# A hybrid S5, short convolution and attention layer on one core: S5 yields given other lengths, q and k requested by the work in front of them

## The chip, the core and the metric

The kernel runs on one core of a Trainium2 chip. The engines that matter here are TensorE (PE in the rows; PEld is its loading of weights), VectorE (DVE), ScalarE (ACT), GpSimd (POOL) and SyncE (SP, which here mostly starts DMAs). Each engine takes its own list of instructions in order and waits on semaphores for what the others make. The metric is device time in microseconds (us) of one execution, lower is better. TensorE's clock is granted at one of two levels, 1.2 or 2.4 GHz; the profile shows the mean of a stretch as PEclk, 1.00 for the upper level.

## The reference

One layer over 1024 tokens of width 1024, in float32:

```python
def hybrid_layer(x, ...):
    h = rmsnorm(x, g_pre_mix)
    proj = jnp.einsum('bld,dn->bln', h, w_in)          # 1024 -> 6664 columns
    u_s5, x_conv, b_conv, c_conv, q, k, v, f_logit, gate_logits = split(proj)
    y_a = s5_mixer(u_s5, ...)            # 32 groups x 16 channels, 64 complex states each
    y_b = gate_b * conv3_causal(gate_c * x_in)
    y_c = forgetting_attention(q, k, v, f_logit, b_f)  # 8 heads x 64, blocks of 128 queries
    gates = jax.nn.sigmoid(gate_logits + b_gate)       # 3 x 1024 columns
    merged = sum over the three branches of gate * (y @ its rows of w_branch)
    x = x + rmsnorm(merged @ w_out, g_post_mix)
    h = rmsnorm(x, g_pre_mlp)
    return x + rmsnorm(square(relu(h @ w_ff1)) @ w_ff2, g_post_mlp)

def s5_mixer(u, ...):
    states = associative_scan(a_bar, b_bar * u)        # complex, over the tokens
    y = gelu(Re(c * states) + d_skip * u)
    return y * sigmoid(y @ w_glu)
```

## The kernel before

Everything that TensorE multiplies from float32 is split by `split` (L71) into a high and a low part in the type fp32r: ScalarE copies the high part, VectorE subtracts it (the copy at L73 and the subtraction at L65 in the rows), and `mm3` multiplies three pairs (high with high, high with low, low with high), each one a product of 128x512 at L122. A projection tile (128 columns of `w_in`) is 2 halves of tokens x 8 blocks of depth x `mm3`, 48 products.

The order of TensorE's work is written by a small planner in Python that runs while the kernel is built. Chains of dependent work are generators (`s5_all` for the S5 branch, `attention`, `forget`, `w2_sums`); where one `yield`s a number, it asks to be called again after so many modelled microseconds. `clk` is a modelled clock, moved on by each matmul that is issued. `run_with` (L106) calls whichever chain is due, and fills in between with one step of `proj_stream` (L263), which is one `mm3` of a projection tile. A modelled `mm3` lasts 0.64. The tiles stand in the queue `todo`: first 12 of the short convolution (cx, cc and cb for each of four blocks j), then 22 gate tiles (g0 to g21), then what is put at its head while the program goes on. The first steps of a tile's stream ask SP for the weights of the tiles behind it, and `nxt.split()` splits the next tile's weight between the steps of this one: `if nxt is not None and (th, kt) == (0, 5):` (L285).

The S5 branch is done in four quarters j of 8 groups (`s5_quarter`, L700 to L825). In one quarter: `Bt` is made of small products by VectorE and GpSimd (Bx) and added up; eight transposes of it (pm, L126) give Mi; `CA` is made in the same way with Cx; `pk` multiplies Bb with CA and gives, through Kq and DMAs, Wi; GpSimd then makes the tables TR and TI of the next quarter (`s5_tables`; those of quarter 0 are asked for ahead of the first quarter); `px` multiplies Mi with U; VectorE makes X of px and of the tables TR and TI, then the scans Z (eight instructions); ScalarE copies Z to Zs; VectorE makes S of Z, Zs and the tables; `py` multiplies CA with S and Wi with U; after a gelu (G1, gq) `pz` multiplies, and so goes to memory as `ya_s`. The yields between them set how much filler stands ahead of each step:

```python
yield SY * (3.9 if j else 9.0)     # L723, ahead of Bt's sum and pm
yield SY * (3.9 if j else 13.0)    # L740, ahead of CA's sum and pk
yield SY * 15.0                    # L790, ahead of py
```

When the quarters are done, what is left of the convolution and one gate tile is issued, then v (pv, the weights of v split by hand), and then the attention. Its 64 units are 4 pairs of heads (hp) x 2 heads x 8 blocks of queries; each has its scores (ps), a softmax on VectorE and ScalarE (P), transposes (pt, to PT), and for every second block the product with v (av). Between these stand the fillers that are left. The q and k tiles of the next pair are put at the head of `todo` by `request_qk`, and the planner issues them behind the last scores of the pair in front (`ready` in `proj_stream`):

```python
if n % 16 == 12 and hp < 3:        # L1114
    request_qk(hp + 1)
```

Beside the attention run GpSimd's sums of `w_ff2` (`w2_sums`), with a row of DMAs on SP. In this stage SP keeps the program's order. Outside the stages that are marked as scheduled by hand, the compiler's scheduler may reorder the instructions of each engine.

Of the kernel before, what the change touches and what calls it, by code (L numbers as in the profile page):

```python
# [38 lines left out]
def hybrid_layer(ctx, tc, a, out, dbg=None):  # L39
# [24 lines left out]
    def tt(o, x, y, op, eng=None):  # L64
        (eng or dve).tensor_tensor(o, x, y, op=op)  # L65
# [27 lines left out]
    clk = [0.0]  # L93
# [4 lines left out]
    def spawn(gen, delay=0.0):  # L98
        heapq.heappush(events, (clk[0] + delay, seq[0], gen))
        seq[0] += 1  # L100

    def poll():
        while events and events[0][0] <= clk[0]:
            _, _, gen = heapq.heappop(events)
            d = next(gen, None)
            if d is not None:  # L106
                spawn(gen, d)
# [146 lines left out]
    def proj(tl, th):  # L254
        wh, wl = tl.split()
        ps = pp.tile([P, HALF], F, name=f"p_{tl.name}{th}", tag="pj", bufs=2)
        for kt in range(KT):
# [2 lines left out]
                tl.cons(th, ps)  # L260
            yield

    def proj_stream():  # L263
        nxt = None
        while True:
            if nxt is None and not todo:
                yield DONE
                continue
            cur = nxt if nxt is not None else todo.popleft()
            cur.split()  # L270
            nxt = todo.popleft() if todo else None
            if nxt is not None:
                nxt.raw.get()
                if cur.name in ahead_of:
                    ahead_of[cur.name].get()
                elif todo:
                    todo[0].raw.get()
            while cur.ready is not None and not cur.ready():
                if not events:
                    raise RuntimeError("stuck")  # L280
                clk[0] = max(clk[0], events[0][0])
                poll()
            for th in range(2):
                for kt, _ in enumerate(proj(cur, th)):
                    if nxt is not None and (th, kt) == (0, 5):  # L285
                        nxt.split()
                    yield


# [381 lines left out]
    SY = 1  # L671
# [28 lines left out]
    def s5_quarter(j):  # L700
# [17 lines left out]
        for s in range(T):  # L718
# [1 line left out]
            e2 = pii[:, T - 1 - s, gs].unsqueeze(2).to_broadcast([P, 8, H])  # L720
            tt(Bt[:, :, s, :], Bb[:, gs, :], e1, MUL)
            tt(Bx[:, :, s, :], Bb2[:, gs, :], e2, MUL, pool)
        yield SY * (3.9 if j else 9.0)  # L723
        tt(Bt, Bt, Bx, ADD)
        yield SY * 2.4
        Mi = q4("Mi", "D")
# [8 lines left out]
        for tau in range(T + 1):  # L735
# [1 line left out]
            e2 = pii2[:, tau, gs].unsqueeze(2).to_broadcast([P, 8, H])  # L737
            tt(CA[:, :, tau, :], C1t[:, gs, :], e1, MUL)
            tt(Cx[:, :, tau, :], C2t[:, gs, :], e2, MUL, pool)
        yield SY * (3.9 if j else 13.0)  # L740
        tt(CA, CA, Cx, ADD)
        yield SY * 2.4

# [43 lines left out]
        tt(Zs[:, :, 0:nv], Zs[:, :, 0:nv], TI[:, :, 0:nv], MUL)  # L787
        tt(S[:, :, 1:P], S[:, :, 1:P], Zs[:, :, 0:nv], SUB)

        yield SY * 15.0  # L790
        py = pp.tile([P, 8, P], F, name=f"py{j}", tag="s", bufs=2)
        for g in range(8):
            mm(py[:, g, :], CA[:, g, 1:T + 1, :].rearrange("p t h -> p (t h)"),
# [98 lines left out]
    for grp in (1, 0):  # L892
        n = 264 if grp else 256
# [131 lines left out]
    def request_qk(hp):  # L1025
        tl = tiles(f"q{hp}", [(C_Q + hp * P, P), (C_K + hp * P, P)], 2, qk_cons(hp),
                   ready=lambda: sdone.get(hp - 1, False))
        todo.extendleft(reversed(tl))

    def attention():  # L1030
# [3 lines left out]
        def scores(u):  # L1034
            hp, e, qb = u
            h = 2 * hp + e
            Q1, Q2, K1, K2 = QK[hp, e]
            kend = (qb + 1) * P
            nch = 1 if kend <= 512 else 2
            cw = kend // nch  # L1040
            mw = max(256, cw)
            qs = slice(qb * P, (qb + 1) * P)
            ps = pp.tile([P, 2, 512], F, name=f"ps{h}{qb}", tag="s", bufs=2)
            for c in range(nch):
                ks = slice(c * cw, c * cw + mw)
                last = c == nch - 1
                mm(ps[:, c, 0:mw], Q1[:, qs], K1[:, ks], True, False, 0.000417 * mw)
                mm(ps[:, c, 0:mw], Q2[0:68, qs], K2[0:68, ks], False, not last, 0.000417 * mw)
                if last:
                    mm(ps[:, c, cw - P:cw], identb, maskb, False, True, 0.06)  # L1050
            sv = ps[:, 0:nch, 0:cw]
            mx = at.tile([P, 1], F, name=f"mx{h}{qb}", tag="mx", bufs=4)
            dve.tensor_reduce(mx, sv, axis=mybir.AxisListType.XY, op=MAX, negate=True)  # L1053
            Pm = Pms[u] = at.tile([P, L], F, name=f"P{h}{qb}", tag="P", bufs=3)
            sm = at.tile([P, 1], F, name=f"sm{h}{qb}", tag="sm", bufs=4)
            act.activation(Pm[:, 0:kend].rearrange("p (c n) -> p c n", c=nch), sv, AF.Exp,  # L1056
                           bias=mx, accum_out=sm)
            dve.reciprocal(sm, sm)
            ts(Pm[:, 0:kend], Pm[:, 0:kend], sm, MUL)
# [43 lines left out]
                av_(u)  # L1103

        prev = None
        for n, u in enumerate(units):
            hp = u[0]
            if n % 16 == 0:
                if hp == 0:
                    request_qk(0)  # L1110
                while not sdone.get(("qk", hp)):
                    yield 1.3
                yield 4.0
            scores(u)  # L1114
            if n % 16 == 15:
                sdone[hp] = True
            yield FILL_A
            if prev is not None:
                yield from tail(prev)
            if n % 16 == 12 and hp < 3:  # L1120
                request_qk(hp + 1)
            prev = u
        yield 3.0
        yield from tail(prev)
# [743 lines left out]
    for i in range(0, KC, 2):  # L1868
        nxt = [p.prep_a for p in pairs[i + 2:i + 4]] if i + 2 < KC else [s_[0] for s_ in stages[:AH]]
# [65 lines left out]
```

## Time and profile before

| | us |
|---|---|
| three runs | 1651.32, 1644.12, 1651.83 |
| median | 1651.32 |
| the profiled execution | 1648.08 |
| span of its instructions | 1646.3 |
| TensorE busy | 1603.7 (97%) |
| VectorE busy | 1033.7 (63%) |
| ScalarE busy | 702.9 (43%) |
| GpSimd busy | 460.8 (28%) |

All times in the rows count from the start of the span. The four S5 quarters lie between about 90 and 350 us, v behind them, the attention between about 460 and 815, and the branch products, the output projection and the MLP after it. In a row of instructions, "x8" is the number of like instructions put together, and the bracket at the end is the idle time of the engine just before, with what ended it.

### The profile page before, as it was taken

Reading aid. Unit: us, or ns where it says so; the run is one execution under the profiler, and the core shown is the slowest. Engines: PE = TensorE matmul, PEld = TensorE weight load, DVE = VectorE, ACT = ScalarE, POOL = GpSimd, SP = SyncE. Lnnn points to the kernel's source line nnn. Section 1 sums busy time; section 2 is a strip of 40 time slices with the busy share of each in tenths; the row PEclk is TensorE's granted clock in tenths of the full one; section 3 lists DMA queues with packets and bytes.
Section 4 is the critical chain, followed back from the end, with each engine's and each line's share of the span. In section 5 each row is a group of like instructions: output and inputs, shape, how many; then the busy total and the mean of one; then the engine's idle time right before and its main releaser. Section 6 shows DMA issues by size and latency. Waiting matters only on the chain.

```text
span 1646.3 us, 20948 instructions
## 1 busy us (share of the span) xinstructions
PE 1603.7 (97%) x7783; PEld 1322.8 (80%) x7783; DVE 1033.7 (63%) x1543; ACT 702.9 (43%) x1060; POOL 460.8 (28%) x578
## 2 busy tenths in 40 slices
PE   7999999999999999999999989999999999999997
PEld 6778888889878888777887768888788878888886
DVE  4768666524156463677682874978887674545665
ACT  6223233322254454566343344744445454443442
POOL 1087844100231413120002314444433200101232
PEclk9999999999999999999999999999999999999999
DMA  5412323332463526441873672456554699665521
GB/s 166 125 46 77 105 76 111 91 103 64 145 214 111 196 96 202 131 167 62 282 253 110 216 241 90 149 173 198 184 175 146 202 344 358 236 202 187 186 88 51
DMA packets 186034, 261.73 MB, mean 159 GB/s; under 512 B 24752, under 2 KB 108764, under 8 KB 183884
## 3 DMA queue, kind: packets, MB, share of 16 engines
q1 hardware_dynamic: 170380, 228.93, 43.2%
q10 hardware_dynamic: 15552, 31.46, 5.1%
q8 instruction: 61, 1.00, 0.2%
q14 instruction: 41, 0.34, 0.1%
HBM read 183.54 MB, written 75.63 MB: 157 GB/s over the span
## 4 chain that ended last, share of the span: by engine, by line
PE 42%; DVE 7%; issue 3%; DMA 3%; ACT 3%; POOL 2%; SPq 0%; DVEq 0%; ACTq 0%; POOLq 0%
PE P L122 13%; PE P4f L122 3%; PE P6f L122 3%; PE P7f L122 3%; PE P5f L122 3%; PE P2f L122 3%; PE P3f L122 3%; PE P1f L122 2%; PE wl L122 2%; PE p_g L122 2%; DVE sa L65 1%; PE p_q L122 1%; PE ps L122 1%; PE av L122 1%; PE pt L126 1%
## 5 line engine op out<-in xcount | busy, mean ns | idle before, releaser
L65 DVE TENSOR_TENSOR st<-x,st 128x1024 fp32r<-128x1024 f32 x70 | 86.8, 1251 | 78.5 <-ACT st L73 77.0
L122 PE MATMUL p_g<-hT,w_g_1H 128*128 128x512 f32 x384 | 125.6, 403 | 0.0
L122 PE MATMUL p_g<-hT,w_g_0H 128*128 128x512 f32 x384 | 124.2, 401 | 1.2 <-ACT K L1019 1.2
L73 ACT ACTIVATE st<-x 128x1024 fp32r<-128x1024 f32 x70 | 73.6, 1059 | 99.0 <-PE P6f L122 16.6
L65 POOL TENSOR_TENSOR w2s<-w2s 128x512 f32<-128x512 f32 x32 | 44.5, 1390 | 215.7 <-DMA w2s<-in_w_ff 188.4
L65 POOL TENSOR_TENSOR s<-w1r 128x512 f32<-128x512 f32 x32 | 53.8, 1701 | 145.5 <-DMA w1r<-in_w_ff 114.9
L65 DVE TENSOR_TENSOR sl<-x,sh 128x1024 fp32r<-128x1024 f32 x42 | 56.6, 1352 | 47.4 <-ACT sh L73 47.4
L122 PEld LDWEIGHTS p_g<-hT,w_g_0H 128*128 128x128 f32 x384 | 69.7, 189 | 13.5 <-ACT K L1019 1.6
L122 PE MATMUL pb<-yH,wb_0L 128*128 128x512 f32 x192 | 75.5, 393 | 3.6 <-DVE wb_0L L65 3.6
L122 PEld LDWEIGHTS p_g<-hT,w_g_1H 128*128 128x128 f32 x384 | 69.4, 190 | 11.6 <-issue 0.2
L122 PE MATMUL p_g<-hT,w_g_1L 128*128 128x512 f32 x192 | 75.8, 395 | 0.0
L122 PE MATMUL p_g<-hT,w_g_0L 128*128 128x512 f32 x192 | 75.5, 393 | 0.0
L65 POOL TENSOR_TENSOR fa<-fa,gfin 128x512 f32<-128x512 f32 x16 | 25.5, 1604 | 178.3 <-ACT fjk L1762 178.3
L122 PE MATMUL pb<-yH,wb_0H 128*128 128x512 f32 x192 | 75.2, 392 | 0.0
L122 PE MATMUL pb<-yL,wb_0H 128*128 128x512 f32 x192 | 74.8, 390 | 0.0
L65 DVE TENSOR_TENSOR PT<-pt,PT 128x512 fp32r<-128x512 f32 (+2 forms) x96 | 53.1, 553 | 28.9 <-ACT PT L73 28.4
L73 ACT ACTIVATE PT<-pt 128x512 fp32r<-128x512 f32 (+2 forms) x96 | 46.9, 489 | 53.5 <-PE pt L126 52.4
L73 ACT ACTIVATE sh<-x 128x1024 fp32r<-128x1024 f32 x42 | 44.2, 1058 | 51.4 <-PE P3f L122 9.9
L1056 ACT ACTIVATE P<-ps,mx 128x128 f32<-128x128 f32 (+3 forms) x64 | 47.3, 739 | 28.1 <-DVE mx L1053 28.0
L1053 DVE TENSOR_REDUCE mx<-ps 128x1 f32<-128x128 f32 (+3 forms) x64 | 48.1, 751 | 13.6 <-PE ps L122 13.3
L862 ACT ACTIVATE g<-p_g,bgcol 128x512 f32<-128x512 f32 x48 | 32.8, 682 | 45.8 <-PE p_g L122 45.3
L126 PE MATMUL pt<-ident,P 128*128 128x128 f32 x288 | 48.7, 278 | 3.0 <-DVE PT L65 2.3
(810 smaller groups left out, 4568.0 us busy)
## 6 DMA issues: line engine op xcount, KB each, us to landing
w2s<-in_w_ff SPq DMA_DIRECT2D x16, 1024.0 KB
w1r<-in_w_ff SPq DMA_DIRECT2D x16, 1024.0 KB
as<-sa SPq DMA_DIRECT2D x16, 1024.0 KB
x<-as SPq DMA_DIRECT2D x32, 512.0 KB
x<-t_P SPq DMA_DIRECT2D x32, 512.0 KB
r_g<-in_w_in SPq DMA_DIRECT2D x12, 1024.0 KB
gt_s<-g ACTq DMA_DIRECT2D x48, 256.0 KB
t_P<-w2s SPq DMA_DIRECT2D x48, 256.0 KB
```

What stands on the lines that cost most here:

```text
L65: (eng or dve).tensor_tensor(o, x, y, op=op)
L73: act.activation(hi, src, AF.Copy, scale=scale)
L122: pe.matmul(o, l, r, start=start, stop=stop)
L126: pe.transpose(o, i, idn)
L862: act.activation(g, ps, AF.Tanh, bias=bgcol[:, i:i + 1], scale=0.5)
L1053: dve.tensor_reduce(mx, sv, axis=mybir.AxisListType.XY, op=MAX, negate=True)
L1056: act.activation(Pm[:, 0:kend].rearrange("p (c n) -> p c n", c=nch), sv, AF.Exp, bias=mx, accum_out=sm)
```

## The change

Four places are edited. The yield ahead of pm is 15.0 instead of 9.0 in quarter 0; that ahead of pk is 8.0 instead of 13.0 in quarter 0 and 1.5 instead of 3.9 in the others; that ahead of py is 10, 15, 13 and 11 in quarters 0 to 3 instead of 15 in each. `proj_stream` splits the weight of a next tile that has a `ready` condition and a raw weight of its own (a q tile behind a gate tile) in its second half of tokens instead of its first. And the attention measures how long its own units last in the modelled clock, and requests q and k when the filler that is left in the tile at hand and the next one (`ahead_us`) is as long as the units that are still to come in the pair.

```diff
@@ -260,6 +260,8 @@
                 tl.cons(th, ps)
             yield
 
+    ahead_us = [0.0]
+
     def proj_stream():
         nxt = None
         while True:
@@ -280,10 +282,12 @@
                     raise RuntimeError("stuck")
                 clk[0] = max(clk[0], events[0][0])
                 poll()
+            late = nxt is not None and nxt.ready is not None and nxt.raw is not cur.raw
             for th in range(2):
                 for kt, _ in enumerate(proj(cur, th)):
-                    if nxt is not None and (th, kt) == (0, 5):
+                    if nxt is not None and (th, kt) == ((1, 0) if late else (0, 5)):
                         nxt.split()
+                    ahead_us[0] = 0.64 * (15 - 8 * th - kt + 16 * (nxt is not None))
                     yield
 
 
@@ -720,7 +724,7 @@
             e2 = pii[:, T - 1 - s, gs].unsqueeze(2).to_broadcast([P, 8, H])
             tt(Bt[:, :, s, :], Bb[:, gs, :], e1, MUL)
             tt(Bx[:, :, s, :], Bb2[:, gs, :], e2, MUL, pool)
-        yield SY * (3.9 if j else 9.0)
+        yield SY * (3.9 if j else 15.0)
         tt(Bt, Bt, Bx, ADD)
         yield SY * 2.4
         Mi = q4("Mi", "D")
@@ -737,7 +741,7 @@
             e2 = pii2[:, tau, gs].unsqueeze(2).to_broadcast([P, 8, H])
             tt(CA[:, :, tau, :], C1t[:, gs, :], e1, MUL)
             tt(Cx[:, :, tau, :], C2t[:, gs, :], e2, MUL, pool)
-        yield SY * (3.9 if j else 13.0)
+        yield SY * (1.5 if j else 8.0)
         tt(CA, CA, Cx, ADD)
         yield SY * 2.4
 
@@ -787,7 +791,7 @@
         tt(Zs[:, :, 0:nv], Zs[:, :, 0:nv], TI[:, :, 0:nv], MUL)
         tt(S[:, :, 1:P], S[:, :, 1:P], Zs[:, :, 0:nv], SUB)
 
-        yield SY * 15.0
+        yield SY * (10.0, 15.0, 13.0, 11.0)[j]
         py = pp.tile([P, 8, P], F, name=f"py{j}", tag="s", bufs=2)
         for g in range(8):
             mm(py[:, g, :], CA[:, g, 1:T + 1, :].rearrange("p t h -> p (t h)"),
@@ -1103,6 +1107,7 @@
                 av_(u)
 
         prev = None
+        dur, asked, t0 = {}, {}, 0.0
         for n, u in enumerate(units):
             hp = u[0]
             if n % 16 == 0:
@@ -1111,14 +1116,20 @@
                 while not sdone.get(("qk", hp)):
                     yield 1.3
                 yield 4.0
+                t0 = clk[0]
             scores(u)
             if n % 16 == 15:
                 sdone[hp] = True
             yield FILL_A
             if prev is not None:
                 yield from tail(prev)
-            if n % 16 == 12 and hp < 3:
+            k = n % 16
+            if k < 8:
+                dur[k] = clk[0] - t0
+            elif hp < 3 and not asked.get(hp) and (k == 15 or ahead_us[0] >= sum(dur[q] for q in range(k - 7, 7))):
+                asked[hp] = True
                 request_qk(hp + 1)
+            t0 = clk[0]
             prev = u
         yield 3.0
         yield from tail(prev)
```

Of the products that stand as filler between the steps of S5, there are, from one step to the next, in the two kernels (counted in TensorE's order):

| quarter | up to pm | pm to pk | pk to px | px to py | py to pz |
|---|---|---|---|---|---|
| 0, before | 12 | 72 | 24 | 102 | 48 |
| 0, now | 36 | 51 | 24 | 78 | 48 |
| 1, before | 48 | 33 | 9 | 102 | 33 |
| 1, now | 48 | 21 | 9 | 102 | 33 |
| 2, before | 48 | 33 | 9 | 102 | 33 |
| 2, now | 48 | 21 | 9 | 93 | 33 |
| 3, before | 48 | 33 | 9 | 102 | 33 |
| 3, now | 48 | 21 | 9 | 84 | 33 |

(up to pm: from the pz of the quarter in front, in quarter 0 from the start of the stage.) Between the last pz and the first pv stand 123 products before and 111 now. The 96 that are missing are issued in the attention, in its third pair of heads.

On TensorE, around the first transposes of Bt (pm0), among the products of the convolution tile cc of block 0, before: p_cc0_00 is the first half of the tokens.

```order
L122 MATMUL p_cc0_00_1103<-hT000_172,w_cc0_0H_1062 128x512
L122 MATMUL p_cc0_00_1103<-hT100_173,w_cc0_0H_1062 128x512
L122 MATMUL p_cc0_00_1103<-hT000_172,w_cc0_0L_1063 128x512
L126 MATMUL pm0_1114<-ident_66,Bt0_1016 128x128 x8
L122 MATMUL p_cc0_00_1103<-hT001_174,w_cc0_0H_1062 128x512
L122 MATMUL p_cc0_00_1103<-hT101_175,w_cc0_0H_1062 128x512
L122 MATMUL p_cc0_00_1103<-hT001_174,w_cc0_0L_1063 128x512
```

The same place of the changed kernel, where p_cc0_01 is the second half of the tokens:

```order
L122 MATMUL p_cc0_01_1135<-hT010_176,w_cc0_0H_1062 128x512
L122 MATMUL p_cc0_01_1135<-hT110_177,w_cc0_0H_1062 128x512
L122 MATMUL p_cc0_01_1135<-hT010_176,w_cc0_0L_1063 128x512
L126 MATMUL pm0_1149<-ident_66,Bt0_1016 128x128 x8
L122 MATMUL p_cc0_01_1135<-hT011_178,w_cc0_0H_1062 128x512
L122 MATMUL p_cc0_01_1135<-hT111_179,w_cc0_0H_1062 128x512
```

The transposes have moved from behind the fourth block of depth of the tile's first half to the same place in its second half, 24 products later.

On VectorE, from X to S of quarter 0, before (w_cx is the low part of the next convolution tile's weight, Bt that of quarter 1):

```order
L65 TENSOR_TENSOR X_1361<-px_1351,TI_954 64x1024 x2
L65 TENSOR_TENSOR X_1360<-px_1351,TR_953 128x1024
L65 TENSOR_TENSOR X_1360<-X_1360,X_1361 128x1024
L777 SCALAR_TENSOR_TENSOR Z_1388<-r_505,X_1360 128x128 x8
L65 TENSOR_TENSOR w_cx_0L<-r_cx_1427,w_cx_0H 128x1024
L65 TENSOR_TENSOR S_1415<-Z_1388,TR_953 128x8x127
L65 TENSOR_TENSOR Zs_1397<-Zs_1397,TI_954 128x8x127
L65 TENSOR_TENSOR Bt_1652<-Bb,prr 128x8x16
L65 TENSOR_TENSOR S_1415<-S_1415,Zs_1397 128x8x127
```

The same stretch of the changed kernel:

```order
L65 TENSOR_TENSOR X_1364<-px_1354,TI_954 64x1024 x2
L65 TENSOR_TENSOR X_1363<-px_1354,TR_953 128x1024
L65 TENSOR_TENSOR X_1363<-X_1363,X_1364 128x1024
L65 TENSOR_TENSOR w_cx_0L<-r_cx_1427,w_cx_0H 128x1024
L781 SCALAR_TENSOR_TENSOR Z_1391<-r_505,X_1363 128x128 x8
L65 TENSOR_TENSOR S_1418<-Z_1391,TR_953 128x8x127
L65 TENSOR_TENSOR Bt_1624<-Bb,prr 128x8x16 x5
L65 TENSOR_TENSOR Zs_1400<-Zs_1400,TI_954 128x8x127
L65 TENSOR_TENSOR Bt_1624<-Bb,prr 128x8x16
L65 TENSOR_TENSOR S_1418<-S_1418,Zs_1400 128x8x127
```

The split of w_cx has moved from behind the scans Z to ahead of them, and five small products of Bt more stand between the two parts of S.

On TensorE, late in the third pair of heads, before: the scores ps51 (head 5, second block of queries) and what follows.

```order
L122 MATMUL ps50_6147<-maskb_73,identb_71 128x128
L122 MATMUL ps51_6196<-K1_21_5665,Q1_21_5664 128x256
L122 MATMUL ps51_6196<-K2_1_3773,Q2_1_3772 128x256
L122 LDWEIGHTS identb_71
L122 MATMUL ps51_6196<-maskb_73,identb_71 128x128
L122 MATMUL p_q3_00_6386<-hT000_172,w_q3_0H_6311 128x512
L122 MATMUL p_q3_00_6386<-hT100_173,w_q3_0H_6311 128x512
L122 MATMUL p_q3_00_6386<-hT000_172,w_q3_0L_6312 128x512
```

The last scores of that pair in the changed kernel, and what follows:

```order
L122 LDWEIGHTS identb_71
L122 MATMUL ps57_6322<-maskb_73,identb_71 128x128
L122 MATMUL p_g20_10_6281<-hT001_174,w_g20_1H_6123 128x512
L122 MATMUL p_g20_10_6281<-hT101_175,w_g20_1H_6123 128x512
L122 MATMUL p_g20_10_6281<-hT001_174,w_g20_1L_6124 128x512
```

Here gate products (g20_1) stand beside the scores to the last one, and q of the fourth pair begins behind them; before it began behind the second block of head 5. From the start of the fourth pair on the orders of all engines are the same but for SP, which asks for the first branch weight (r_wb) one round of the w2 sums later.

## Rows read from the trace of the kernel before

**Rows 1.** The head of the page: span, and busy time, share of the span and instructions of each engine.

```profile
span 1646.3 us, 20948 instructions
PE 1603.7 (97%) x7783; PEld 1322.8 (80%) x7783; DVE 1033.7 (63%) x1543; ACT 702.9 (43%) x1060; POOL 460.8 (28%) x578
```

**Rows 2.** Busy time by stretch: the stretch and its length, then busy us and instructions of PE, PEld, DVE, ACT and POOL, the granted clock, the DMA share and GB/s.

```profile
90.00:101.00 11.00, 7.22 (x25) 5.76 (x24) 6.35 (x11) 1.25 (x2) 11.00 (x30) 0.69 0.05 12
101.00:347.00 246.00, 245.46 (x1249) 206.51 (x1248) 150.87 (x186) 68.99 (x83) 131.36 (x215) 1.00 0.31 88
554.00:650.00 96.00, 95.31 (x506) 77.78 (x505) 52.98 (x94) 47.85 (x94) 28.94 (x20) 1.00 0.44 155
650.00:726.00 76.00, 73.67 (x409) 59.54 (x408) 48.78 (x92) 42.10 (x88) 16.86 (x12) 1.00 0.50 154
```

**Rows 3.** TensorE's instructions in order of time, 90 to 102 us: start, us of the group, engine, line, operation, out<-in, tile, count, and in the bracket the idle time before it.

```profile
90.13 0.39 PE L122 MATMUL p_cc<-hT,w_cc_0L 128*128 128x512 f32 x1
94.29 1.94 PE L126 MATMUL pm<-ident,Bt 128*128 128x128 f32 x8 [3.78 <-DVE Bt L65]
95.88 1.20 PE L122 MATMUL p_cc<-hT,w_cc_0H 128*128 128x512 f32 x2
...
99.87 0.63 PE L122 MATMUL p_cc<-hT,w_cc_0H 128*128 128x512 f32 x2
...
100.57 0.62 PE L122 MATMUL p_cc<-hT,w_cc_0H 128*128 128x512 f32 x2
...
101.26 0.62 PE L122 MATMUL p_cc<-hT,w_cc_0H 128*128 128x512 f32 x2
```

**Rows 4.** Busy time by stretch, with the columns of rows 2, of short stretches in which the clock was low.

```profile
90.00:94.00 4.00, 0.52 (x3) 0.09 (x1) 1.22 (x2) 0.00 (x0) 4.00 (x14) 0.88 0.00 0
94.00:97.00 3.00, 2.71 (x11) 2.54 (x12) 3.00 (x7) 0.73 (x1) 3.00 (x7) 0.50 0.00 0
970.00:975.00 5.00, 3.04 (x8) 2.40 (x8) 4.99 (x8) 1.46 (x2) 0.00 (x0) 0.53 0.85 305
```

**Rows 5.** VectorE's instructions in order of time, quarter 0.

```profile
92.91 1.23 DVE L65 TENSOR_TENSOR Bt<-Bt,Bx 128x1024 f32<-128x1024 f32 x1 [2.79 <-POOL Bx L65]
...
105.38 1.60 DVE L65 TENSOR_TENSOR CA<-CA,Cx 128x1152 f32<-128x1152 f32 x1 [6.25 <-POOL Cx L65]
...
123.87 2.46 DVE L65 TENSOR_TENSOR X<-px,TI 64x1024 f32<-64x1024 f32 x2
...
132.76 1.23 DVE L65 TENSOR_TENSOR w_cx_0L<-r_cx,w_cx_0H 128x1024 fp32r<-128x1024 f32 x1 [0.95 <-ACT w_cx_0H L73]
...
137.04 1.20 DVE L65 TENSOR_TENSOR S<-S,Zs 128x1016 f32<-128x1016 f32 x1
```

**Rows 6.** GpSimd's instructions in order of time: the last of the table TI of quarter 0 and of quarter 2.

```profile
120.62 2.13 POOL L65 TENSOR_TENSOR TI<-pt 128x512 f32<-128x512 f32 x1
...
263.30 1.28 POOL L65 TENSOR_TENSOR TI<-pt 128x512 f32<-128x512 f32 x1
```

**Rows 7.** TensorE's instructions in order of time, the steps of quarter 0 behind pm.

```profile
114.29 1.92 PE L122 MATMUL pk<-CA,Bb 128*16 128x128 f32 x16
116.14 0.73 PE L122 MATMUL p_cb<-hT,w_cb_0H 128*128 128x512 f32 x2
...
121.72 1.95 PE L122 MATMUL px<-U,Mi 128*128 128x128 f32 x16
123.43 0.71 PE L122 MATMUL p_cx<-hT,w_cx_0H 128*128 128x512 f32 x2
...
146.66 0.38 PE L122 MATMUL py<-S,CA 128*128 128x128 f32 x2
```

**Rows 8.** VectorE's and TensorE's instructions in order of time: scans, S and the start of py of quarter 1, then of quarter 2.

```profile
200.77 5.32 DVE L777 TENSOR_TENSOR_SCAN Z<-r,X 128x128 f32<-128x128 f32 x8
...
209.68 1.21 DVE L65 TENSOR_TENSOR S<-S,Zs 128x1016 f32<-128x1016 f32 x1
...
211.28 0.38 PE L122 MATMUL py<-S,CA 128*128 128x128 f32 x2
...
256.80 8.37 DVE L777 TENSOR_TENSOR_SCAN Z<-r,X 128x128 f32<-128x128 f32 x8
...
268.71 1.21 DVE L65 TENSOR_TENSOR S<-S,Zs 128x1016 f32<-128x1016 f32 x1
...
273.31 0.38 PE L122 MATMUL py<-S,CA 128*128 128x128 f32 x2
```

**Rows 9.** Waits of TensorE, 60 to 460 us: what waited and what it waited for, then the total, the number of times, the longest.

```profile
PE pm L126 <- DVE Bt L65: 4.3, 2, 3.8
...
PE pv L122 <- ACT g L862: 0.8, 1, 0.8
```

**Rows 10.** VectorE's instructions in order of time, third pair of heads.

```profile
657.34 2.27 DVE L65 TENSOR_TENSOR w_q_0L<-r_q,w_q_0H 128x1024 fp32r<-128x1024 f32 x1 [3.66 <-ACT w_q_0H L73]
```

**Rows 11.** TensorE's instructions in order of time, at the same place.

```profile
661.70 0.66 PE L126 MATMUL pt<-ident,P 128*128 128x128 f32 x4 [1.50 <-DVE PT L65]
```

## The prediction

> **What bounds the kernel now.** I read the first table of the page, then the stretches, then the waits of TensorE, and last the instructions around each wait. TensorE (PE) is busy for 1603.7 of the 1646.3 us span [rows 1], so the kernel is a stream of matmuls, and a change that takes none away can only win or lose PE's idle time and its slow-clock time. The profiled execution took 1648.08 us, 1.8 us more than its span; the sum below is made against it. The three timed runs have a median of 1651.32, 3.2 us above it, and spread from 1644.1 to 1651.8, so I put the forecast half of that difference (1.6 us) above the sum. A difference under 0.5% (8.3 us) is about what a measurement of this kernel can't tell from none.
>
> The stretches show where PE isn't full [rows 2]. From 101 to 347 us (the S5 quarters) it lacks 0.5 of 246 us: every S5 step lies behind enough filler. From 90 to 101 it lacks 3.8 of 11, and the granted clock there is 0.69. In the attention, the second head pair (554 to 650) lacks 0.7 us and the third (650 to 726) 2.3. These are the only places in reach of the change.
>
> **The change, part by part.** All 96 products leave the four S5 quarters and come back in the third head pair; PE's work is the same. One product (128x512) takes 0.23 us: three of them go from 100.57 to 101.26 [rows 3].
>
> *The first transposes.* PE has its last filler product at 90.13 and so is free at 90.36; it idles 3.78 us, until Bt (92.91 + 1.23 = 94.14, [rows 5]) is there at 94.29 [rows 3]. In that idle time the granted clock falls: 0.88 in 90 to 94, 0.50 in 94 to 97 [rows 4], which is 1.2 instead of 2.4 GHz. The eight transposes then take 1.59 us instead of some 0.8, and the three triples from 95.88 to 99.87 take 3.99 instead of 3 x 0.69 = 2.07. So this place costs 3.8 + 0.8 + 1.9 = 6.5 us. With 24 products more in front (the order shows 36 instead of 12) PE arrives at 90.36 + 24 x 0.23 = 95.9, 1.7 us after Bt. The wait goes and the slow clock with it: **-6.5 us**. VectorE and GpSimd do the same things in the same order up to here, so nothing later takes the wait's place.
>
> *What is late next: the first py.* Counting fillers in the order of the change: transposes 95.9 to 96.7, 51 products, the pk matmuls at 108.4 (their CA is ready at 105.38 + 1.60 = 106.98 [rows 5], so there is no wait), 1.85 us of them, 24 products, px at 115.8 to 117.5, 78 products, py at 135.4. Before, these were 114.29, 121.72 and 146.66 [rows 7]; S, which py needs, was ready at 137.04 + 1.21 = 138.25 [rows 5], and py had 8.4 us in hand. One would move S forward by the 5.9 us that px moves, and find 3 us left. But the first thing done with px on VectorE (X) also reads the table TI of that quarter, and GpSimd writes TI last at 120.62 to 122.75 [rows 6]. GpSimd is busy without a gap from 90 to 101 [rows 2], and its order hardly changes, so TI comes at 122.8 again; X started at 123.87, only 1.1 us after it [rows 5]. From X to S it took 14.4 us. In the new order the split of the next conv weight (1.23 us, at 132.76 before) stands ahead of the scan Z and not beside ScalarE's copy of Z, and five small Bt products stand between the two S steps (some 1.5 us), in time that was partly idle. So X gains 1.0 and the chain loses about 1: S again at 138.2, and PE waits 138.2 - 135.4 = **+2.8 us**. Bounds: 0 if X starts at 117.5 without the table, 4 if the inserted work adds all of its 2.7. I take 2.8, since TI's row fixes the start of X.
>
> The page "GPSIMD Engine Reference" of the Trainium skill (section 1, Specifications) says that GpSimd shares its SBUF interfaces with VectorE and contends with VectorE instructions that have two SBUF inputs. The same write of TI took 2.13 us at 120.62 and 1.28 at 263.30 [rows 6], which agrees. By that rule the conv products, which now run some 3 us earlier beside the table, would keep TI at 122.75 or later and the wait at 2.8 to 3.5; without it TI could end 0.85 us earlier and the wait would be 2.0.
>
> *The other py.* Quarter 1 keeps its 102 products, and py had 211.28 - (209.68 + 1.21) = 0.4 us in hand [rows 8]. The new order starts Z about 2 us sooner, puts a conv product (1.2 us) between the last steps of S, and lets Z run beside more of the table of quarter 2; the eight scans took 5.32 us in quarter 1 and 8.37 in quarter 2 [rows 8]. That is a wait of -0.4 to +3; I take 1.0. Quarter 2 loses 9 products (2.1 us) of 273.31 - (268.71 + 1.21) = 3.4 in hand, and a weight split that waits for a gate tile now holds Z some 2 us longer: a wait of 0 to 3, I take 0.5. Quarter 3 loses 18 and had the most; 0. Together **+1.5 us**, bounds 0 and 6. The pk steps of quarters 1 to 3 lose 12 products each (2.8 us); CA there follows pm by about 3 us on GpSimd and VectorE, and pk still comes 5.6 us after pm: 0.
>
> *Small ones.* Of PE's 4.3 us on Bt, 3.8 are the first transposes; the other 0.5, in quarter 2, goes because the conv steps between so and Bt are gone there. The 0.8 us of pv on a gate tile [rows 9] go because pv is no longer broken by gate products. **-1.3 us**, bounds -1.3 and 0.
>
> *The attention.* In the third pair q and k of the last pair stood among the scores, and their weights were split early: w_q_0L holds VectorE from 657.34 for 2.27 us, and pt waits 1.50 us behind it until 661.70 [rows 10, 11]. The changed order gives this pair gate products between the scores, and q and k in one block behind them, as the second pair has them. The second pair idles 0.7 us where the third idles 2.3: **-1.6 us**, bounds -2.3 (all of it) and +1 (the two more gate weights are split here, each 1.06 on ScalarE and 1.23 on VectorE in front of a softmax step). The later split of q's weight (at the second half of the gate tile ahead) moves it by three steps of three products and is in this. SP gets q, k and the gate weights in another order and asks for the first branch weight one round of w2 sums later; in the changed kernel the last scores lie further ahead of the next pair, which pays for that round: 0.
>
> Sum: -6.5 + 2.8 + 1.5 - 1.3 - 1.6 = -5.1, so 1648.1 - 5.1 = 1643.0 in the profile's terms and, 1.6 above, **1645 us**.
>
> **The rivals.**
> *No new waits* (0.24). If X doesn't have to wait for TI, the margins read off the trace (8.4, 3.4 and more) cover the fillers taken, and only the gains stand: 1643.0 - 4.3 + 1.6 = 1640. For it: every quarter after the first shows idle VectorE time that could absorb the reordering. Against it: TI's row.
> *The clock falls at the new wait* (0.22). The idle time at 90.5 lowered the clock within 4 us [rows 4]; a wait of 2.8 us at py may do the same, and the work behind it would lose the same 2.7 us: 1647. For it: the clock also was 0.53 at 970 to 975, among broken waits. Against it: the third pair's 1.5 us wait left the clock at 1.00 [rows 2]. The page "TensorE: Matmul & The Clock Gate" of the Trainium skill (Part 1) has the same mechanism: an idle TensorE is gated to half its clock, and activity releases it. The trace agrees at 94 to 97.
> *S5 becomes the bound* (0.12), the slower end. With less filler the chain X, Z, S of VectorE, slowed by GpSimd's tables, ends after PE's arrival in quarters 0, 1 and 2. At the upper bounds these are 4, 4 and 3 us, and 2.7 us of slow clock behind each: 11 + 8 = 19 instead of the 4.3 counted, which makes 1643.0 + 14.8 + 1.6 = 1659. For it: py of quarter 1 has 0.4 us in hand now. Against it: quarters 2 and 3 keep 1 us or more by the rows. It decides from two py waits of over 3 us each.
>
> **How the numbers follow.** Forecast 0.42, with its own range 1640 to 1650; the rivals 0.24, 0.22 and 0.12. Faster by over 0.5% means under 1643.1: most of the first rival (0.19) and a fifth of the forecast (0.09), 0.28. Slower means over 1659.6 by the median, or over 1656 by the profile; nearly all of the last rival: 0.11. Within 0.5%: 0.61. The range runs from 1638, under the first rival, to 1655, between the second and the third; it leaves out the slower end and the low tail.
>
> **What would show it.** Right: no PE wait before the first pm and a clock of 1.00 from 90 to 101; the first X on VectorE starting at 122 to 124, as now, though px ends near 117.5; a PE wait of about 2 to 4 us on S ahead of the first py; PE idling under 1 us in the third pair. Wrong: X starting right behind px (then 1640), or PE at half clock behind py (1647), or waits over 3 us at two py.

## The result, and the profile after

The changed kernel takes 1656.94 us (median of 12 runs, 1655.0 to 1662.1) where the kernel before takes 1649.68 (12 runs): a ratio of 1.0050, interval 1.0039 to 1.0061. It is slower by 7 us, where 1645 was forecast. Each ratio compares runs of a kernel with runs of the kernel before taken side by side; two runs far out (2006 us of e2 and 5682 us of e3 below) count in their medians and not in the ratios. The profiled execution took 1657.67 us, and all stage sums below are of one profiled execution of each kernel.

The head of the page, with the columns of rows 1: the span is 9.6 us longer, and PE is busy for 6.4 us more though it does the same matmuls.

```profile
span 1655.9 us, 20945 instructions
PE 1610.1 (97%) x7783; PEld 1328.3 (80%) x7783; DVE 1031.7 (62%) x1543; ACT 704.6 (43%) x1060; POOL 456.8 (28%) x578
```

Busy time by stretch of the changed kernel, with the columns of [rows 2]:

```profile
90.00:101.00 11.00, 11.00 (x54) 9.21 (x53) 6.69 (x13) 2.92 (x4) 11.00 (x31) 1.00 0.03 4
101.00:347.00 246.00, 235.35 (x1180) 197.04 (x1179) 151.32 (x188) 65.65 (x79) 132.20 (x218) 0.98 0.30 84
...
136.00:140.00 4.00, 0.34 (x1) 0.37 (x2) 4.00 (x6) 0.49 (x1) 3.84 (x5) 0.83 0.00 0
140.00:146.00 6.00, 6.00 (x32) 6.00 (x32) 0.76 (x2) 0.00 (x0) 5.61 (x8) 0.54 0.00 0
269.00:272.00 3.00, 3.00 (x15) 3.00 (x16) 0.10 (x1) 0.00 (x0) 0.00 (x0) 0.54 0.02 5
650.00:726.00 76.00, 75.23 (x408) 61.35 (x407) 42.85 (x80) 37.03 (x75) 15.58 (x12) 1.00 0.48 153
```

The stretch from 90 to 101 is full and at full clock, where [rows 2] had 7.22 of 11 us at 0.69. The S5 quarters behind it lack 10.7 of 246 us instead of 0.5, and behind two of the waits the clock is at its lower level (0.54 over a stretch is near 0.50, 1.2 GHz).

TensorE in order of time: the first transposes, then the starts of py in quarters 0, 1 and 2, with the rows in front of them.

```profile
96.13 1.04 PE L126 MATMUL pm<-ident,Bt 128*128 128x128 f32 x8
...
135.36 0.39 PE L122 MATMUL p_cc<-hT,w_cc_0L 128*128 128x512 f32 x1
139.66 0.76 PE L122 MATMUL py<-S,CA 128*128 128x128 f32 x2 [3.91 <-DVE S L65]
...
205.22 0.72 PE L122 MATMUL p_cx<-hT,w_cx_0H 128*128 128x512 f32 x2 [2.06 <-ACT bs L852]
208.21 0.46 PE L122 MATMUL py<-S,CA 128*128 128x128 f32 x2 [0.64 <-DVE S L65]
...
268.85 0.77 PE L122 MATMUL py<-S,CA 128*128 128x128 f32 x2 [3.71 <-DVE S L65]
```

The wait of [rows 3] at pm is gone, and three places have taken over: 3.91, 2.06 + 0.64 and 3.71 us. What holds S is read on VectorE. Quarter 0, from CA to S:

```profile
105.74 1.60 DVE L65 TENSOR_TENSOR CA<-CA,Cx 128x1152 f32<-128x1152 f32 x1 [6.25 <-POOL Cx L65]
...
116.50 1.21 DVE L65 TENSOR_TENSOR ac<-ac,bs 128x1024 f32<-128x1024 f32 x1
124.50 2.46 DVE L65 TENSOR_TENSOR X<-px,TI 64x1024 f32<-64x1024 f32 x2 [6.80 <-POOL TI L65]
...
129.39 1.26 DVE L65 TENSOR_TENSOR w_cx_0L<-r_cx,w_cx_0H 128x1024 fp32r<-128x1024 f32 x1
130.57 3.07 DVE L781 TENSOR_TENSOR_SCAN Z<-r,X 128x128 f32<-128x128 f32 x8
...
138.31 1.20 DVE L65 TENSOR_TENSOR S<-S,Zs 128x1016 f32<-128x1016 f32 x1
```

VectorE stands idle for 6.80 us until GpSimd has made TI; px had ended at 118.05. On GpSimd one of the table's steps took 3.24 us (the other five of its size 1.04 to 1.29), beside the split and the convolution step that VectorE now does earlier (115.36 to 117.71), and TI ended at 124.46 where it had ended at 122.75 [rows 6]:

```profile
115.37 3.24 POOL L65 TENSOR_TENSOR pt<-TR,wr 128x512 f32<-128x512 f32 x1
...
123.18 1.28 POOL L65 TENSOR_TENSOR TI<-pt 128x512 f32<-128x512 f32 x1
```

Quarter 1, from X to S, and below it quarter 2, from X to the scans Z:

```profile
185.82 1.45 DVE L65 TENSOR_TENSOR X<-X,X 128x1024 f32<-128x1024 f32 x1
187.75 1.23 DVE L65 TENSOR_TENSOR w_cc_0L<-r_cc,w_cc_0H 128x1024 fp32r<-128x1024 f32 x1 [0.47 <-ACT w_cc_0H L73]
188.89 1.64 DVE L65 TENSOR_TENSOR vp<-vp,xs 128x1024 f32<-128x1024 f32 x1
190.57 0.99 DVE L60 TENSOR_SCALAR ac<-vp,cwcol 128x1024 f32<-128x1024 f32 x1
191.59 3.63 DVE L68 SCALAR_TENSOR_TENSOR ac<-vp,cwcol,ac 128x1024 f32<-128x1024 f32 x2
195.14 7.18 DVE L781 TENSOR_TENSOR_SCAN Z<-r,X 128x128 f32<-128x128 f32 x8
...
205.71 1.22 DVE L65 TENSOR_TENSOR ac<-ac,bs 128x1024 f32<-128x1024 f32 x1
206.85 1.21 DVE L65 TENSOR_TENSOR S<-S,Zs 128x1016 f32<-128x1016 f32 x1
...
249.50 1.58 DVE L65 TENSOR_TENSOR X<-X,X 128x1024 f32<-128x1024 f32 x1
255.84 1.81 DVE L65 TENSOR_TENSOR w_g_1L<-r_g,w_g_1H 128x1024 fp32r<-128x1024 f32 x1 [4.77 <-ACT w_g_1H L73]
257.57 6.38 DVE L781 TENSOR_TENSOR_SCAN Z<-r,X 128x128 f32<-128x128 f32 x8
```

The same in the kernel before, quarter 1 and below it quarter 2:

```profile
188.99 2.46 DVE L65 TENSOR_TENSOR X<-px,TI 64x1024 f32<-64x1024 f32 x2
192.72 1.28 DVE L65 TENSOR_TENSOR X<-X,X 128x1024 f32<-128x1024 f32 x1
197.39 1.23 DVE L65 TENSOR_TENSOR w_cb_0L<-r_cb,w_cb_0H 128x1024 fp32r<-128x1024 f32 x1 [3.39 <-ACT w_cb_0H L73]
198.53 2.32 DVE L65 TENSOR_TENSOR ac<-ac,bs 128x1024 f32<-128x1024 f32 x1
...
253.97 1.24 DVE L65 TENSOR_TENSOR w_g_1L<-r_g,w_g_1H 128x1024 fp32r<-128x1024 f32 x1
255.13 1.64 DVE L65 TENSOR_TENSOR X<-X,X 128x1024 f32<-128x1024 f32 x1
```

In quarter 1 X is ready at 187.3, and the scans begin at 195.1, behind a weight split and a whole convolution block. Before, that block stood ahead of X, and another split and one convolution step stood between X and the scans (194.0 to 200.8, [rows 8]). So this gap grew only from 6.8 to 7.9 us; the scans took 7.18 us instead of 5.32, beside more of GpSimd's table, and one convolution step (1.22 us) now stands among the steps of S. From the start of X to S it is 26.0 us instead of 21.9. In quarter 2 X is ready at 251.1, and the scans stand behind a split that waits 4.77 us for ScalarE; before, the same split didn't wait, and the scans followed X at once (256.80, [rows 8]). The 2.06 us of quarter 1 on "ACT bs" are the same delay by another way. ScalarE, in order of time:

```profile
192.32 0.60 ACT L852 ACTIVATE bs<-p_cb 128x512 f32<-128x512 f32 x1 [4.12 <-PE p_cb L122]
202.42 1.06 ACT L784 ACTIVATE Zs<-Z 64x1024 f32<-64x1024 f32 x1 [9.50 <-DVE Z L781]
203.49 1.05 ACT L785 ACTIVATE Zs<-Z 64x1024 f32<-64x1024 f32 x1
204.57 0.60 ACT L852 ACTIVATE bs<-p_cb 128x512 f32<-128x512 f32 x1
```

Zs waits 9.50 us for the scans, and bs, which frees the filler's PSUM buffer, stands behind it in ScalarE's list. So late scans stop the filler too.

To add up stages I use one number worked out from all of TensorE's rows: the time from each matmul's start to the next one's, less the 30th percentile of that time for its shape (0.227 us for 128x512). This excess holds waits and slow clock together. From 75 to 350 us it is 9.9 before and 19.4 after, from 450 to 800 us (the attention) 21.3 and 22.3, and in the rest 30.1 and 29.0. The S5 quarters alone make the whole loss: -6.6 at pm0, +7.0 at py0, +3.4 around py1, +5.4 at py2.

### The profile page after: what moved, and what is told of

The parts are those of the page before. It is cut to its first block, busy times and chain, and to the rows that moved or that the text cites. A ratio compares the mean times of both kernels' runs of the same rounds, so it can differ in the third digit from the quotient of the medians.

```text
span 1655.9 us, 20945 instructions
## 1 busy us (share of the span) xinstructions
PE 1610.1 (97%) x7783; PEld 1328.3 (80%) x7783; DVE 1031.7 (62%) x1543; ACT 704.6 (43%) x1060; POOL 456.8 (28%) x578
## 4 chain that ended last, share of the span: by engine, by line
PE 71%; DVE 13%; issue 5%; ACT 4%; POOL 4%; DMA 2%; SPq 0%; DVEq 0%; ACTq 0%; POOLq 0%
PE p_g L122 14%; PE P L122 12%; PE p_q L122 4%; PE p_u L122 3%; PE P4f L122 3%; PE P7f L122 3%; PE P3f L122 3%; PE P6f L122 3%; PE P5f L122 3%; PE P2f L122 3%; PE pv L122 2%; PE P1f L122 2%; PE av L122 2%; PE wl L122 2%; PE ps L122 2%
## 5 line engine op out<-in xcount | busy, mean ns | idle before, releaser
L65 POOL TENSOR_TENSOR fa<-fa,gfin 128x512 f32<-128x512 f32 x16 | 25.5, 1605 | 178.2 <-ACT fjk L1773 178.2
```

## The experiments

The last two columns are counted in each kernel's order and worked out as above: filler products from the first scores of the third pair of heads to those of the fourth (the 96 of q and k of the fourth pair among them), and the excess in S5 and in the attention.

| kernel | median us | ratio to before (95%) | products, third pair | S5 | attention |
|---|---|---|---|---|---|
| before | 1649.68 | | 165 | 9.9 | 21.3 |
| changed | 1656.94 | 1.0050 (1.0039 to 1.0061) | 267 | 19.4 | 22.3 |
| e1 | 1655.50 | 1.0027 (1.0015 to 1.0040) | 120 | 2.4 | 39.7 |
| e2 | 1656.43 | 1.0026 (1.0012 to 1.0040) | 165 | 11.0 | 32.7 |
| e3 | 1652.12 | 1.0014 (1.0004 to 1.0023) | 171 | 10.3 | 27.9 |
| e4 | 1652.99 | 1.0017 (1.0008 to 1.0027) | 171 | 9.8 | 28.3 |
| e5 | 1657.65 | 1.0038 (1.0025 to 1.0051) | 267 | 19.9 | 22.6 |
| e6 | 1658.06 | 1.0057 (1.0035 to 1.0080) | 261 | 20.9 | 20.6 |
| e7 | 1660.58 | 1.0057 (1.0045 to 1.0069) | 261 | 21.3 | 20.8 |
| e8 | 1649.08 | 0.9989 (0.9980 to 0.9998) | 165 | 9.8 | 25.5 |
| e9 | 1645.33 | 0.9979 (0.9969 to 0.9989) | 267 | 10.7 | 19.3 |
| e10 | 1644.75 | 0.9971 (0.9961 to 0.9981) | 165 | 7.7 | 21.8 |
| e11 | 1654.07 | 1.0023 (1.0013 to 1.0033) | 120 | 5.7 | 32.7 |
| e12 | 1650.17 | 1.0005 (0.9995 to 1.0015) | 165 | 9.7 | 24.8 |

In e2, e3 and e4 the percentile for 128x512 comes out one nanosecond lower (0.226), which puts about 1 us too much into each of their two sums. Differences of that size between rows say nothing.

**e1: the kernel before, with the first yield alone.**

```diff
-        yield SY * (3.9 if j else 9.0)
+        yield SY * (3.9 if j else 15.0)
```

> The kernel before with one edit, the yield of 15.0 ahead of the first transposes. My theory, that the loss of the full change lies in quarters 0 to 2 between px and py (scans Z and S come late) and not at the first transposes: no TensorE wait at pm0 and full clock there, 6.5 us less than before at that place; py0 still has its 102 products behind px, so no wait there; the DVE order now has a gate or convolution split ahead of the scans in quarters 1 and 2, which may cost 0 to 2 us: 1643 to 1646 us against 1649.7. Rival, that any moving of the S5 steps against the convolution tiles costs what it gains: 1649 or more.

S5 does as forecast: 7.5 us less excess, no py waits. But the time is that of the rival, for a reason that neither had: the products that S5 now takes are missing in the third pair, where 120 are left of 165 and the excess of the attention rises by 18 us (TensorE busy for 66.8 of the 80 us from 640). Its longest wait there is 5.24 us at a pt, with the lower clock behind it, where q's split had made ScalarE wait 4.52 us for r_q. In e11, which loads r_q earlier, that wait is gone and 11 us of the 18 are left.

**e2: the changed kernel with all S5 yields of before.** Its edit is the attention's part of the change.

> The changed kernel with all S5 yields as before, so that only the request of q and k and the later split are left. My theory: the S5 part is that of before (excess over the ideal stream from 75 to 350 us about 10 us, of which 6.8 at pm0), the attention is worth between -1.5 and +1.6 us: 1648 to 1651.5. Rival, that the dense block of q and k or the changed order of the weights in the attention makes the slowdown: 1654 or more.

By its median the attention's part alone costs nearly as much as the whole change (1656.43 against 1656.94), by its ratio about half (1.0026 against 1.0050). It lies in the attention, whose excess rises by 10 to 11 us. The load of the last q and k weight (SyncE), q's split on ScalarE and TensorE's wait, each row from its own engine in order of time:

```profile
662.32 1.56 SPq L1156 DMA_DIRECT2D t_P<-w2s  x2
663.98 1.14 SPq L231 DMA_DIRECT2D r_q<-in_w_in  x2
...
668.49 1.06 ACT L73 ACTIVATE w_q_0H<-r_q 128x1024 fp32r<-128x1024 f32 x1 [6.03 <-DMA r_q<-in_w_in]
...
671.46 1.97 PE L122 MATMUL av<-PT,V 128*128 128x256 f32 x8 [5.90 <-DVE PT L65]
```

The request falls later than by the old rule, and r_q stands on SyncE behind the stores t_P of a w2 round instead of in front of them; in the kernel before it was issued at 649.97. The split stands early in ScalarE's list and holds the softmax until the weight has landed.

**e3 and e4: the changed kernel with the pk yields, or the py yields, of before.**

```diff
-        yield SY * (1.5 if j else 8.0)                # e3
+        yield SY * (3.9 if j else 13.0)
-        yield SY * (10.0, 15.0, 13.0, 11.0)[j]        # e4
+        yield SY * 15.0
```

> The changed kernel with the two pk yields of before (13.0 and 3.9), py yields as changed. My theory A, that px 12 products earlier (21 in quarter 0) against the convolution and gate tiles puts their VectorE work ahead of the scans: py0 is reached 24 products later (5.5 us), after S, no wait and no slow clock (-7.0 us); quarter 1 has the VectorE order of before, its wait falls from 2.7 to under 1; quarter 2 has a split of a gate weight ahead of the scans that was before the same number in the order of before, wait 0 to 2: 1643 to 1648 us. Theory B, that the shorter py yields are what leaves TensorE waiting: quarters 2 and 3 still wait, 3 us or more each at py, 1652 or more.

> The changed kernel with the py yield of before (15.0), pk yields as changed. Theory A: py0 has 24 products more, TensorE arrives at about 141.2 us and S is ready at 139.5, no wait; quarter 1, whose number of products ahead of py isn't changed by this edit, still waits 1 to 3 us; quarter 2 has 9 products more (2.1 us) and still waits 1 to 2 us of its 3.7: 1644 to 1649 us. Theory B: with the py yields back all waits of py go, quarter 1 too: 1640 to 1644.

Either edit takes away the wait at py0 (S is ready 2.06 and 1.91 us ahead). In quarter 1, e3 has VectorE's order and time of before (21.9 us from X to S); e4, with as many products ahead of py1 as the changed kernel, waits only 0.68 us (p_cc), with its convolution block among the steps of X and 22.6 us from X to S instead of 26.0: there VectorE's order counts, not the number. At py2 e3 waits 1.29 and e4 under 0.5; e3's split ahead of the scans even waits 6.49 us, but the scans then run beside only the last step of GpSimd's table and take 3.71 us instead of 6.38. The times (1652.12 and 1652.99) still miss theory A's ranges, and e3's lies where theory B had it, without B's waits at py. What A left out is a new wait at pz0 (2.90 and 2.64 us, each with a slow clock behind it) and r_q behind a w2 round as in e2 (4.05 and 4.78 us at a pt).

**e5: TI of quarter 0 finished on VectorE.**

```diff
+            if j == 0 and e == 6:
+                ev = dve          # and a scratch tile of its own
```

> The changed kernel, with the last half of the table TI of quarter 0 made on VectorE in a buffer of its own (three instructions of about 1.2 us, in the 6.8 us that it waits for GpSimd before X), beside GpSimd's last half of TR. Theory: X of quarter 0 waits for TI and nothing else; X then starts at 120 to 122 us instead of 124.5, S is ready at about 136.3 instead of 139.5, TensorE's wait at py0 falls from 3.9 us to under 1 and its clock stays up: 6 to 7 us less, 1649 to 1652 against 1656.9. Rival, that the other VectorE work between X and S (the split of w_cx, the small Bt products) sets S: the wait stays at 3 us or more, 1655 to 1657.

The time (1657.65) is about the rival's, and my theory that X waits for TI and nothing else falls. VectorE, GpSimd, VectorE:

```profile
111.56 1.42 DVE L65 TENSOR_TENSOR TI<-ptd 128x512 f32<-128x512 f32 x1
...
113.96 2.13 POOL L65 TENSOR_TENSOR TR<-pt 128x512 f32<-128x512 f32 x1
...
123.12 2.46 DVE L65 TENSOR_TENSOR X<-px,TI 64x1024 f32<-64x1024 f32 x2
```

Both tables are there at 116.1, 8.4 us sooner, and X starts only 1.4 us sooner: the convolution block that stood in front of the idle time has been pushed behind the table work and now fills VectorE up to X. The wait at py0 grew to 5.95 us. Between CA and S VectorE's own work almost fills the time.

**e6 and e7: splits and convolution results held behind the last scan; e7 with e5's edit too.**

```diff
-        yield SY * 2.6     # between X and the scans
+            zi[0] = dve.tensor_tensor_scan(...)
+                with behind():          # tc.issue_after(zi[0].ins)
+                    self.w = wsplit(...)
```

> The changed kernel, with the yield between X and the scans taken out (2.6 more ahead of py for it) and all weight splits and results of the convolution that are issued later held behind the last scan on VectorE. Theory: in quarters 1 and 2 py waits because this work stands ahead of the scans; with the scans right behind X the waits at py1 and py2 (2.7 and 3.7 us, and 1.7 of slow clock behind the second) go, and S of quarter 0 comes 1.3 us sooner: 7 to 9 us less, 1648 to 1650. Rival, that the held splits come too late for TensorE's products and the wait only changes its name (p_c or p_g on a split): 1655 or more.

> Both edits in one. Theory: the waits of all four py go, the excess over the ideal stream from 75 to 350 us falls from 19.4 to 3 to 6 us, and with the attention as in the changed kernel the time is 1640 to 1645 us, under both kernels. Rival, that S5 gains are given back in the attention because the requests of q and k now fall at other places of SyncE's order: 1648 or more.

The rival of e6 holds. The waits at py0 and py2 are gone (py1 still waits 2.42 us), and the weights are late instead; TensorE in e6:

```profile
130.89 0.79 PE L127 MATMUL p_cc<-hT,w_cc_0L 128*128 128x512 f32 x1 [4.53 <-DVE w_cc_0L L65]
...
259.90 0.80 PE L127 MATMUL p_g<-hT,w_g_1L 128*128 128x512 f32 x1 [3.77 <-DVE w_g_1L L65]
```

Whichever comes second on VectorE is late. In e7 the two edits don't add up (p_cc waits 5.69 us), and there was no gain in S5 that the attention could have taken back, as its rival had it.

**e8: e2 with the q and k weight loaded at the request.**

```diff
         todo.extendleft(reversed(tl))
+        tl[0].raw.get()
```

> The kernel of run e2_attn_only with one line more: the load of the raw q and k weight is issued at the moment of the request, so that it stands ahead of a round of w2 sums on SyncE instead of behind it. Theory: in e2 the load started at 664.0 us, behind four stores that wait for GpSimd, and the split of q, early in ScalarE's order, held the softmax for 6 us; with the load at about 651 the wait of 5.9 us and the slow clock behind it (2.3 us) go: 1647 to 1650 against 1656.4. Rival, that the thin filler of the third pair is what costs: the loss moves to other waits in the pair, 1654 or more.

The time is as expected: r_q is issued at 652.40, ahead of the round, and 1656.43 becomes 1649.08. The wait falls from 5.90 to 2.63 us and doesn't go; the slow clock behind it does. Busy time by stretch (columns of [rows 2]), e2 and then e8:

```profile
640.00:716.00 76.00, 70.05 (x366) 56.62 (x364) 39.98 (x78) 36.41 (x76) 15.18 (x12) 0.96 0.42 132
```

```profile
640.00:716.00 76.00, 72.70 (x395) 58.73 (x394) 45.73 (x87) 40.77 (x85) 16.90 (x12) 1.00 0.47 147
```

**e9: less convolution work on VectorE; branch B is left out.**

```diff
-                    tt(vp[:, 2:], vp[:, 2:], cvt["xs"], MUL)
-                    stt(ac, vp[:, 1:L + 1], cwcol[:, 4 + j:5 + j], ac, MUL, ADD)
-                    stt(ac, vp[:, 2:L + 2], cwcol[:, 8 + j:9 + j], ac, MUL, ADD)
```

> The changed kernel without three of the four VectorE steps of each convolution block (the product with x and the second and third tap), so that branch B is not computed. All else on VectorE keeps its order. Theory, that py waits because VectorE's list holds other work in front of and among the steps from px to S: in quarter 1, where 5.3 us of these steps stand between X and the scans, the wait at py (2.7 us) goes; in quarter 2, where the scans stand behind a split of a gate weight, it stays at 3 to 4 us; in quarter 0, where they stand ahead of X and beside GpSimd's table, S comes 0 to 3 us sooner and the wait is 1 to 4 us. Rival, that the number of products ahead of py alone decides: all three waits as in the changed kernel.

TensorE in e9, the starts of py in quarters 0 and 2:

```profile
136.57 0.46 PE L122 MATMUL py<-S,CA 128*128 128x128 f32 x2 [1.78 <-DVE S L65]
...
258.77 0.46 PE L122 MATMUL py<-S,CA 128*128 128x128 f32 x2 [1.75 <-DVE S L65]
```

With the same products ahead of each py, the waits fall to 1.78 us at py0, none at py1 and 1.75 at py2, and S5's excess from 19.4 to 10.7. VectorE's load, not the count of products alone, sets S. At py2 I had expected no gain: the split still waits 4.60 us, but the scans, beside less of GpSimd's table, take 4.53 instead of 6.38. In quarter 0 X starts at 120.38, 4.1 us sooner (all of this quarter runs some 0.9 us ahead), since GpSimd's table too is done sooner: its six steps of 128x256, beside fewer VectorE steps, take 6.2 us instead of 8.9. The page "GPSIMD Engine Reference" of the Trainium skill (section 1, Specifications) says that GpSimd contends with VectorE instructions of two SBUF inputs. The trace agrees, by these 2.7 us.

**e10 and e11: py's yield back, pz of quarter 0 later, q and k loaded at the fifth unit; e11 also with 3.9 ahead of pk in quarters 1 to 3.**

```diff
-        yield SY * (10.0, 15.0, 13.0, 11.0)[j]
+        yield SY * 15.0
-        yield SY * (6.5 if j else 10.0)
+        yield SY * (6.5 if j else 13.0)
+            if k == 4 and hp < 3:
+                make_qk(hp + 1)
+                qkt[hp + 1][0].raw.get()
```

> The changed kernel with py's yield at 15.0 in all quarters, the yield ahead of pz of quarter 0 at 13.0 instead of 10.0 (run e4 waited 2.6 us there), and the raw weights of q and k loaded when the fifth unit of the pair in front is done, ahead of the request. Theory: no wait at pm0 and py0, under 1 us at pz0, 1 to 3 us in quarters 1 and 2 together (as in e4), so an excess of 4 to 7 us from 75 to 350 us; the load of the last q lies a round of w2 sums or more ahead of its split, so no 5 us wait in the third pair: 1641 to 1646. Rival, that the attention with 33 products fewer than in the changed kernel is too thin: 1649 or more.

> As run e10, but with the pk yields of before in quarters 1 to 3 (3.9), so that 36 products more stay in S5. Theory: quarters 1 to 3 as in e1, an excess of 2.5 to 4 us from 75 to 350 us, and an attention that is thinner by 36 products: 1641 to 1648. Rival, that the third pair starves as in e1 (15 us more than the changed kernel there) whatever the load of q does: 1652 or more.

e10 beats both kernels, as forecast: 5 us under the one before (ratio 0.9971, interval 0.9961 to 0.9981), some 12 under the changed one. Its S5 stage and its third pair (columns of [rows 2]):

```profile
101.00:347.00 246.00, 241.74 (x1231) 202.74 (x1230) 158.40 (x189) 68.66 (x82) 135.46 (x217) 1.00 0.31 89
640.00:716.00 76.00, 75.91 (x417) 61.31 (x416) 48.97 (x92) 43.15 (x90) 16.95 (x13) 1.00 0.50 157
```

S5 still waits 2.60 us on bs (near pz0, where I had put under 1) and 1.47 at py1, and its excess is 7.7 instead of 4 to 7; r_q is issued at 637.93 and q split at 650.2, without a wait. e11's S5 is better, but its third pair has 120 products again and starves as in e1, though r_q comes early: waits of 1.67 and 2.13 us at pt, and the rival's 1654.

**e12: the kernel before with the later split alone.**

> The kernel before with the later split of q's weight alone; the request as before. Theory: in e2 it was the request by the work in front that put the load of the last q behind a round of w2 sums; with the old request the load starts at about 650 to 654 us, ahead of the round, and the later split takes the 1.5 us wait of before away or leaves it: 1648 to 1651. Rival, that the later split itself costs: 1654 or more, with q's products waiting for their weight (p_q on w_q).

No change (1.0005), r_q at 651.68. So it is the request rule that put r_q behind the round in e2, not the split.

## Why the prediction was wrong

- *The first transposes, -6.5.* Right: 6.6 by the excess, and clock and wait as described.
- *The first py, +2.8.* Its mechanism was right (arrival 135.4 forecast, 135.8 measured; X at 122 to 124, measured 124.5, held by TI), its size was not: TI ended at 124.46 instead of 122.75, behind the GpSimd step of 3.24 us, so S came at 139.5 instead of 138.2, and I had put the slow clock behind the wait into a rival (0.22) though [rows 4] showed it after 3.8 us. The eight pairs of py took 6.6 us instead of 3.7 [rows 7 show their start before; they ended at 150.39]. The place cost 7.0.
- *The other py, +1.5.* This step failed most: 8.8 measured. For quarter 1 I took 1.0 of a range that ended at 3, and it was 3.4: the convolution step late in S (1.2 us) and the scans beside the table (1.9 us longer) were in the range, but I had Z start about 2 us sooner and overlooked the split and the convolution block that the new order puts between X and Z, so that the gap between X and Z is 1.1 us longer instead. For quarter 2 I took 2 us for a split that waits for a gate tile; it was 4.8 + 1.8 us, and a slow clock followed. With quarter 0 this is the mechanism of the slower rival (1659, chance 0.12): waits of 3.9, 2.7 and 3.7 us against its 4, 4 and 3. It decided from two waits of over 3 us, and there were two. Of the 14.7 us between the forecast (-5.1) and the profile (+9.6), this step is 7.3 and the first py 4.2.
- *The pk steps, 0.* pk itself never waits, but its yield moves px, and with it X and the scans, against the filler tiles' work on VectorE and against GpSimd's table: e3 and the changed kernel differ by it alone, and by 9 to 10 us of S5 excess. The 0 looked at pk only.
- *Small ones, -1.3.* Nearly right: the wait of pm2 fell from 0.5 to 0.2 us at most, and pv's from 0.8 to 0.2.
- *The attention, -1.6.* Measured +1.0. In the third pair it came as forecast: TensorE lacks 0.8 us from 650 to 726 instead of 2.3, and pt's 1.5 us wait fell to 0.77. But the last scores wait 1.82 us as they did before (1.84), and now the clock fell behind it (0.79 from 770 to 778, 1.00 before). Why here and not there stays open; the same wait was followed by the lower clock in 10 of the 14 profiled kernels, e12 among them. "SyncE's new order: 0" held in the whole change, where r_q is issued at 647.47, ahead of a w2 round; with 165 products in the pair (e2) r_q stands behind a round, and it costs 6 us at one wait.

## What to carry to other kernels

Filler has a value only up to what the chain beside it needs: the attention gained nothing from 267 products over 165, and lost 11 us (e11) to 18 us (e1) at 120. Before a step is moved against the filler, read the in-order list of the engine that carries the chain: moving px by 12 products put a convolution block behind X that had stood ahead of it, and let the scans run beside more of GpSimd's table. And a load that others queue behind should be asked for by when it must land, not by when its consumer's turn comes.

## What was not expected of the hardware

A short wait can cost nearly twice its length: behind 3.91 us at py0 the clock was 0.54 for 6 us, and the place cost 7.0. The length of a wait alone did not tell whether the clock falls. In the S5 stage waits of 2.64 us and more were all followed by the lower clock, and so were e9's of 1.78 and 1.75; those of 2.42 (e6), 2.57 (e11) and 2.60 (e10) and the 2.06 + 0.64 of the changed kernel were not. Equal GpSimd steps (128x512) took 1.04 to 3.25 us. Eight scans took 2.6 us in quarter 3 of every kernel, where GpSimd has no table to make, and 3.7 to 8.9 in quarters 1 and 2 beside its table.
